# Stream passes that read their tokens from the last to the first, over weight tiles that lie interleaved in pairs

## The chip, the cores and the metric

The kernel runs on one core of a Trainium2 chip. The metric is the device time of one execution in microseconds: the time before is 1301.39 us, the median of three runs (1300.91 to 1302.28).

## The reference

Two layers of a hybrid block over 16 + 256 = 272 tokens of width 1024. Each layer has a mixer (one wide projection, three branches: retention, HGRN2 and differential attention, a gated sum, and an output projection) and a convolutional FFN.

```python
def mixer(hn, w_in, w_branch, w_out, ...):
    proj = (hn @ w_in).astype(F32)             # 1024 -> 13312: the inputs of all branches and the gates
    ...
    o_ret = retention(...); o_hg = hgrn2(...); o_da = diff_attention(...)
    branches = jnp.stack([o_ret, o_hg, o_da], axis=2)
    y_b = jnp.einsum('blnc,ncd->blnd', branches, w_branch.astype(F32))
    gates = jax.nn.sigmoid(mg.reshape(b, l, N_BRANCH, D_MODEL))
    return jnp.sum(gates * y_b, axis=2).astype(hn.dtype) @ w_out

def conv_ffn(hn, w_ffn_in, conv_w, conv_b, w_ffn_out, valid):
    u = jnp.where(valid[None, :, None], hn @ w_ffn_in, 0.0)      # 1024 -> 5632
    ...                                        # a causal convolution of width 3 over tokens
    gate, val = jnp.split(c, 2, axis=-1)
    return (jax.nn.silu(gate) * val) @ w_ffn_out                 # 2816 -> 1024

def reference(x, meta, ...):
    for li in range(DEPTH):                    # 2 layers
        h = h + mixer(rms_norm(h, norm_mix_g[li]), ...)
        h = h + conv_ffn(rms_norm(h, norm_ffn_g[li]), ...)
    return rms_norm(h, norm_final_g)[:, PAD:]
```

Everything is fp32. Nearly all of the arithmetic lies in the products with the weights.

## The kernel before, in words

**The stream.** All weight matrices are cut on the host into tiles of 128 x 128 and laid out in the order in which they are used (`_turns`, `_stream`): 1616 tiles a layer. Eight tiles make a chunk of 512 KB, which one DMA on SP's queue brings into a buffer `wraw` (three of them). ScalarE then rounds the chunk to fp32r (`whi`, four buffers), and VectorE subtracts that from the original to get the rest (`wlo`, four buffers). This is `_Weights.next`. The activations are split in the same way into a high and a low part (`xh`/`xl`, `ghi`/`glo`, `yhi`/`ylo`, `b0hi`/`b0lo` and so on).

**A stream pass.** `products` makes one pair of output column tiles (f = 0 and 1) of a matrix. For each tile it does three matmuls with the weight tile as the stationary operand and the tokens as the moving one (lines 915, 916, 917):

```python
nc.tensor.matmul(o, wh, hi, start=first, stop=False)
nc.tensor.matmul(o, wh, lo, start=False, stop=False)
nc.tensor.matmul(o, wl, hi, start=False, stop=last)
```

Each of them is a weight load of 128 columns (LDWEIGHTS) and a pass of 272 tokens, or of 258 in those parts of the last layer that need no more (`t0` = 14 there). The output `o` lies in PSUM. The two tiles f = 0 and 1 with the same k follow each other in the stream; the exception is the last pair of the first layer's FFN output (`fo`, j = 3), where k follows k. The FFN output of the last layer is computed the other way round: there the weights are the moving operand, 512 wide, and the tokens the stationary one (lines 1520 to 1522).

**Where the tiles lie.** An operand's row k starts at 64 x (k % 4) bytes modulo 256, since a row of 272 tokens has 1088 bytes. `_places` puts each weight tile in its buffer so that its first column, modulo `LINE` = 256 bytes, stands at a set distance `APART` from the operand's row; `APART` has one value for passes of 272 and one for those of 258, and `BLOCK` is added for operands in another kind of buffer. `_runs` joins neighbouring tiles, so that one instruction of ScalarE and one of VectorE does a whole chunk, most often as four runs of 256 columns.

**The order of work.** Every instruction is recorded in a plan (`_Plan`, line 593 is where all recorded calls are issued), and a simulation with fixed costs for each engine orders them once, when the kernel is built. TensorE's stream passes set its clock; the other work (branches, norms, splitting) is spread around them by due times. Most instructions therefore carry line 593 and are told apart by their tiles.

Of the kernel before, what the change touches and what calls it, by code (L numbers as in the profile page):

```python
# [19 lines left out]
P = 128  # L20
DEPTH = 2
# [18 lines left out]
CHUNK_TILES = 8  # L40
# [48 lines left out]
def _ktiles(name):  # L89
    return FK if name == "fo" else KD  # L90


def _turns(li):

    pairs = [x for x in ORDER if x[0][0] not in MARKS]
    if li == DEPTH - 1:
        pairs = [x for x in pairs if x[0] != "fo"]  # L100
    groups = [[x] for x in pairs]
    if li == 0:
        groups[:2] = [pairs[:2]]
    turned = [[pairs[pairs.index((name, 0)) + DEFER - 1]] for name in ("hq", "fi")]
    out = []
    for group in groups:
        if group == [("fo", 3)]:
            out.append([("fo", 3, k, f) for f in range(2) for k in range(FK)])
        else:
            nk = _ktiles(group[0][0])  # L110
            out.append([x + (k, f) for k in range(nk // 2) for x in group for f in range(2)])
            out[-1] += [x + (k, f) for x in group for k in range(nk // 2, nk) for f in range(2)]
            if group in turned:
                out[-1] = out[-1][nk:] + out[-1][:nk]
    if li == DEPTH - 1:
        out.append([("fo", j, k, f) for k in range(FK) for j in range(KD // 2) for f in range(2)])
    return out


STREAM = sum(2 * _ktiles(n) for n, _ in ORDER if n[0] not in MARKS)  # L120


LINE = 256
APART = (0, 200)
BLOCK = 64
ROOM = CHUNK_TILES * P + 2 * LINE // 4
T0 = META - 2
# [3 lines left out]
def _places(depth=DEPTH):  # L131

    wants = []
    for li in range(depth):
        for name, j, k, _ in sum(_turns(li), []):
            if name == "fo" and (li == DEPTH - 1 or j == 3):
                wants.append(None)
                continue  # L140
            short = li == DEPTH - 1 and name not in FULL
            wants.append(APART[short] + BLOCK * (name[0] == "b" or name in ("wo", "fo")) + 64 * (k % 4))
    out = []
    for c in range(0, len(wants), CHUNK_TILES):
        at, places = 0, []
        for want in wants[c : c + CHUNK_TILES]:
            if want is not None:
                at += (want // 4 - at) % (LINE // 4)
            places.append(at)
            at += P  # L150
        assert at <= ROOM
        out.append(places)
    return out


def _runs(places):


    runs = []
    for i, at in enumerate(places):  # L160
        if runs and at == runs[-1][1] + runs[-1][2] * P:
            runs[-1][2] += 1
        else:
            runs.append([i, at, 1])
    out = []
    for i, at, n in runs:
        if out and out[-1][4] == n and (out[-1][3] == 1 or at == out[-1][1] + out[-1][2] * out[-1][3]):
            if out[-1][3] == 1:
                out[-1][2] = at - out[-1][1]
            out[-1][3] += 1  # L170
        else:
            out.append([i, at, 0, 1, n])
    return out
# [22 lines left out]
def _stream(w_in, w_branch, w_out, w_ffn_in, w_ffn_out):  # L196

    out = np.empty((DEPTH, STREAM, P, P), np.float32)
    for li in range(DEPTH):
        tiles = sum(_turns(li), [])  # L200
        for i, (name, j, k, f) in enumerate(tiles):
            if name in BASE:
                w, cols = w_in[li], _columns(name, BASE[name] + 2 * j + f)
            elif name in ("b0", "b1", "b2"):
                w, cols = w_branch[li][int(name[1])], _columns(name, 2 * j + f)
            elif name == "wo":
                w, cols = w_out[li], _columns(name, 2 * j + f)
            elif name == "fi":
                w, cols = w_ffn_in[li], _columns(name, j + f * FK)
            else:  # L210
                w, cols = w_ffn_out[li], _columns(name, 2 * j + f)
            out[li, i] = w[k * P : (k + 1) * P][:, cols]
    n = DEPTH * STREAM // CHUNK_TILES
    out = out.reshape(n, CHUNK_TILES, P, P).transpose(0, 2, 1, 3)
    return np.ascontiguousarray(out).reshape(n, P, CHUNK_TILES * P)
# [382 lines left out]
class _Weights:  # L598
# [13 lines left out]
    def next(self):  # L612
        c, i = divmod(self.used, CHUNK_TILES)
        self.used += 1
        if i == 0:
            due = self.plan.key
            room = [P, ROOM]
            raw = self.plan.tile(self.pool, [P, CHUNK_TILES * P], F32, "wraw", 3, f"wraw{c}")
            hi = self.plan.tile(self.pool, room, F32R, "whi", 4, f"whi{c}")
            lo = self.plan.tile(self.pool, room, F32R, "wlo", 4, f"wlo{c}")  # L620
            self.plan.key = due - LEAD
            pieces = 1 if c > 1 else 2
            for p in range(pieces):
                n = CHUNK_TILES // pieces
                cols = slice(p * n * P, (p + 1) * n * P)
                self.sp.dma_start(raw[:, cols], self.w[c][:, cols])
                for first, at, step, runs, each in _runs(self.places[c][p * n : (p + 1) * n]):
                    src = raw[:, (p * n + first) * P : (p * n + first + runs * each) * P].rearrange("p (r x) -> p r x", r=runs)
                    self.act.activation(self.part(hi, at, step, runs, each), src, AF.Copy)
                    self.dve.tensor_tensor(out=self.part(lo, at, step, runs, each), in0=src, in1=self.part(hi, at, step, runs, each).bitcast(F32), op=SUB)  # L630
            self.plan.key = due
            self.cut = hi, lo
        hi, lo = self.cut
        at = self.places[c][i]
        return hi[:, at : at + P], lo[:, at : at + P]

    def chunk(self):

        for _ in range(CHUNK_TILES):
            self.next()  # L640
        return self.cut


def build(tc, a, depth=DEPTH, probe=None):
# [7 lines left out]
def _trace(ctx, tc, plan, a, depth, probe):  # L652
# [239 lines left out]
    def products(xs, name, j, t0=0):  # L892

        if name in BASE or name == "fi":
            norm.next()
        if ahead:
            return ahead.pop()
        tiles = turns.pop(0)
        main = lambda: new(mp, [P, 2, 512], F32, "main", 2, "main")[:, :, t0:T]
        ps = {i: main() for i in sorted({x[1] for x in tiles})}  # L900
        to = {x: ps[x[0]][:, x[1], :] for x in {x[1::2] for x in tiles}}
        if (name, j) == ("fo", 3):

            to[j, 1] = main()[:, 1, :]
        cost = 3 * ((T - t0) / 2400 + 0.003)
        left = dict.fromkeys(to, _ktiles(name))
        for _, i, k, f in tiles:
            hi, lo = (x[:, t0:] for x in xs(k))
            begun = left[i, f] < _ktiles(name)
            left[i, f] -= 1  # L910
            plan.key = clock[0]
            wh, wl = weights.next()

            def run(o=to[i, f], wh=wh, wl=wl, hi=hi, lo=lo, first=not begun, last=left[i, f] == 0):
                nc.tensor.matmul(o, wh, hi, start=first, stop=False)  # L915
                nc.tensor.matmul(o, wh, lo, start=False, stop=False)  # L916
                nc.tensor.matmul(o, wl, hi, start=False, stop=last)  # L917

            plan.main.append(plan.add("pe", run, cost, [to[i, f]], [wh, wl, hi, lo], count=6))
            clock[0] += cost  # L920
        plan.key = clock[0] - 1.0
        if (name, j) == ("fo", 3):
            return [to[j, f] for f in range(2)]
        ahead.extend(ps[i] for i in ps if i != j)
        return ps[j]
# [71 lines left out]
    for li in range(depth):  # L997
# [546 lines left out]
        for name, j in ORDER:  # L1544
# [18 lines left out]
            elif name[0] == "*":  # L1563
                plan.key = clock[0] - MARGIN
                n = name[1:]
                if n == "b2":
                    blocks = [st["da0"], st["da1"]]
                else:
                    t = st["rg" if n == "b0" else "hg"]
# [4 lines left out]
            two = slice(2 * (j % 2), 2 * (j % 2) + 2)  # L1574
            both = slice(2 * j, 2 * j + 2)
            if name in BASE:
                lo = 0 if name in FULL else t0
# [17 lines left out]
                elif name in ("dq", "dk"):  # L1595
                    t = block(f"{name}{j // 2}")
# [3 lines left out]
                elif name == "rv":  # L1600
# [3 lines left out]
                    src = values(ps, st["rvt"][j // 2], (j % 2) * 2 * P)  # L1604
# [4 lines left out]
                elif name in ("hi", "dv"):  # L1609
                    n = name[0] + "v"  # L1610
# [6 lines left out]
                    src = values(ps, st[f"{n}t{b}"], (j % 2) * 2 * P)  # L1617
# [6 lines left out]
                else:  # L1624
                    t = block(f"{name}{j // 2}")
# [21 lines left out]
            elif name == "wo":  # L1647
                hi, lo = st["yhi"], st["ylo"]
# [11 lines left out]
            elif name == "fi":  # L1660
# [11 lines left out]
                first = META if last else 0  # L1672
                c = temp2("two_b")
                for f in range(2):
# [4 lines left out]
                    for back in (1, 2):  # L1679
                        at = max(first, back)  # L1680
                        stt(c[:, f, at:], u[:, f, at - back - t0 : T - back - t0], w(2 - back), c[:, f, at:], MUL, ADD)
                c = c[:, :, first:]
# [6 lines left out]
            else:  # L1689
                hi, lo = st["ghi"], st["glo"]  # L1690
# [35 lines left out]
```

## Time and profile before

| | |
|---|---|
| median of three runs | 1301.39 us |
| profiled execution, span from its first to its last instruction | 1299.9 us |
| TensorE busy | 1290.8 us (99%) |
| weight loads busy | 1268.7 us (98%) |
| VectorE busy | 993.4 us (76%) |
| ScalarE busy | 855.9 us (66%) |
| GpSimd busy | 85.6 us (7%) |
| DMA | 219.01 MB, mean 168 GB/s |

The profile is of one execution. No time of its own is given for it beside the span; the span is 1.5 us less than the median of the runs. In the rows, PE is TensorE's matmuls, PEld its weight loads, DVE VectorE, ACT ScalarE, POOL GpSimd and SP the engine that issues the weights' DMAs. A group's row has the line, the engine, the operation, output<-inputs, the array's rows x columns, the tile, the count, busy us, the mean ns of one, and the idle time just before. A matmul's duration is longer than the distance to the next one, because matmuls are pipelined: 290 ns and some 125 ns here. A window's row has, for each engine, its busy time and the number of its instructions, then the granted clock, the DMA engines' share and GB/s.

### The profile page before, as it was taken

The numbers are of one execution on the slowest core, as the hardware profiler recorded it, in microseconds if no ns is written. First come the engines' busy times: TensorE is split into PE (matmuls) and PEld (weight loads), VectorE is DVE, ScalarE is ACT, GpSimd is POOL, SyncE is SP. The second block draws the span as 40 slices with busy tenths as digits, with TensorE's granted clock in tenths as the row PEclk, the third lists the DMA queues.
The fourth block names the chain that finished last, engine by engine and source line by source line (L and its number), as shares of the span: only waits on it lengthen the run. The fifth ranks groups of instructions, "written<-read, shape, count | busy, mean of one in ns | idle before, by whom it ended". The sixth has DMA issues, their size and how long they took to land.

```text
span 1299.9 us, 27225 instructions
## 1 busy us (share of the span) xinstructions
PE 1290.8 (99%) x10965; PEld 1268.7 (98%) x10965; DVE 993.4 (76%) x1745; ACT 855.9 (66%) x1490; POOL 85.6 (7%) x162
## 2 busy tenths in 40 slices
PE   9999999999999999999999999999999999999998
PEld 8999999999999999999999999999999999999986
DVE  7685888698686789886565868886997868899753
ACT  6765565766777568776456664657667876787743
POOL 5000000000100020000020000000001100200000
PEclk9999999999999999999999999999999999999999
DMA  8555444435544555555555455454444456556653
GB/s 279 195 159 155 167 149 154 146 136 158 162 143 152 180 161 184 187 173 170 178 179 181 161 171 171 146 172 140 149 161 163 146 163 197 173 186 202 201 183 109
DMA packets 60751, 219.01 MB, mean 168 GB/s; under 512 B 6864, under 2 KB 6992, under 8 KB 60624
## 3 DMA queue, kind: packets, MB, share of 16 engines
q1 hardware_dynamic: 60336, 216.74, 51.6%
q8 instruction: 86, 1.41, 0.4%
q10 hardware_dynamic: 288, 0.52, 0.1%
q14 instruction: 41, 0.34, 0.1%
HBM read 216.19 MB, written 1.05 MB: 167 GB/s over the span
## 4 chain that ended last, share of the span: by engine, by line
PE 95%; DVE 3%; DMA 1%; issue 0%; SPq 0%; POOL 0%; ACT 0%; DVEq 0%
PE main L917 28%; PE main L915 28%; PE main L916 27%; PE fo L1520 2%; PE fo L1522 2%; PE fo L1521 2%; PE ds L1383 1%; PE do L593 1%; PE ro L593 1%; PE ho L593 1%; DMA wraw<-in_w 1%; PE vt L593 1%; DVE wlo L593 1%; PE wt L593 0%; PE lev L1106 0%; PE ms L593 0%
## 5 line engine op out<-in xcount | busy, mean ns | idle before, releaser
L915 PE MATMUL main<-xh,whi 128*128 128x272 f32 (+1 forms) x2368 | 687.8, 290 | 0.7 <-ACT whi L593 0.7
L917 PE MATMUL main<-xh,wlo 128*128 128x272 f32 (+1 forms) x2368 | 679.5, 287 | 0.5 <-DVE wlo L593 0.4
L916 PE MATMUL main<-xl,whi 128*128 128x272 f32 (+1 forms) x2368 | 670.4, 283 | 0.0
L593 DVE TENSOR_TENSOR wlo<-wraw,whi 128x1024 fp32r<-128x1024 f32 (+1 forms) x408 | 496.0, 1222 | 198.7 <-ACT whi L593 195.4
L593 ACT ACTIVATE whi<-wraw 128x1024 fp32r<-128x1024 f32 (+1 forms) x408 | 426.5, 1048 | 214.0 <-PE main L916 137.5
L916 PEld LDWEIGHTS main<-xl,whi 128*128 128x128 f32 x2368 | 449.3, 190 | 0.2
L915 PEld LDWEIGHTS main<-xh,whi 128*128 128x128 f32 x2368 | 445.5, 188 | 2.1 <-ACT whi L593 0.9
L917 PEld LDWEIGHTS main<-xh,wlo 128*128 128x128 f32 x2368 | 444.6, 188 | 1.4 <-DVE wlo L593 1.4
L593 DVE SCALAR_TENSOR_TENSOR two_b<-u,small,two_b 128x256 f32<-128x256 f32 (+2 forms) x176 | 78.3, 485 | 0.7 <-ACT two_b L593 0.2
L593 POOL TENSOR_TENSOR y<-h,rstd 128x272 f32<-128x272 f32 x32 | 38.2, 1225 | 311.1 <-ACT rstd L593 311.1
L917 PE MATMUL main<-ghi,wlo 128*128 128x272 f32 x176 | 51.0, 290 | 0.0
L915 PE MATMUL main<-ghi,whi 128*128 128x272 f32 x176 | 50.8, 288 | 0.0
L916 PE MATMUL main<-glo,whi 128*128 128x272 f32 x176 | 50.2, 285 | 0.0
L593 ACT ACTIVATE two_b<-u,small 128x272 f32<-128x272 f32 (+1 forms) x88 | 49.3, 598 | 0.7 <-DVE glo L593 0.5
L593 ACT ACTIVATE u<-main 128x544 f32<-128x544 f32 (+1 forms) x40 | 24.5, 612 | 36.5 <-PE main L917 36.4
L915 PE MATMUL main<-b0hi,whi 128*128 128x272 f32 (+1 forms) x128 | 37.3, 292 | 0.0
L915 PE MATMUL main<-b1hi,whi 128*128 128x272 f32 (+1 forms) x128 | 37.3, 292 | 0.0
L917 PE MATMUL main<-yhi,wlo 128*128 128x272 f32 (+1 forms) x128 | 36.5, 286 | 0.0
L917 PE MATMUL main<-b2hi,wlo 128*128 128x272 f32 (+1 forms) x128 | 36.5, 285 | 0.0
L917 PE MATMUL main<-b0hi,wlo 128*128 128x272 f32 (+1 forms) x128 | 36.5, 285 | 0.0
L917 PE MATMUL main<-b1hi,wlo 128*128 128x272 f32 (+1 forms) x128 | 36.5, 285 | 0.0
L915 PE MATMUL main<-b2hi,whi 128*128 128x272 f32 (+1 forms) x128 | 36.4, 284 | 0.0
(268 smaller groups left out, 1951.7 us busy)
## 6 DMA issues: line engine op xcount, KB each, us to landing
wraw<-in_w SPq DMA_DIRECT2D x402, 512.0 KB, 3.6
h<-in_h SPq DMA_DIRECT2D x4, 272.0 KB, 5.3
dec<-in_dec SPq DMA_DIRECT2D x2, 544.0 KB, 4.5
wraw<-in_w SPq DMA_DIRECT2D x4, 256.0 KB, 5.0
const<-in_const SPq DMA_DIRECT2D x1, 937.0 KB, 6.8
gain<-in_gl SPq DMA_DIRECT2D x1, 512.0 KB, 5.1
out<-y ACTq DMA_DIRECT2D x2, 256.0 KB, 2.7
out<-y SPq DMA_DIRECT2D x2, 256.0 KB, 2.7
```

Source lines behind the costliest of these rows:

```text
L593: self.plan.add(self.name, lambda: f(*args, **kw), cost, outs, ins, args[2] if method == "activation" else None, count)
L915: nc.tensor.matmul(o, wh, hi, start=first, stop=False)
L916: nc.tensor.matmul(o, wh, lo, start=False, stop=False)
L917: nc.tensor.matmul(o, wl, hi, start=False, stop=last)
L1383: nc.tensor.matmul(ss[m][:, at : at + nk], q[half, hd, q0 : q0 + P], k[half, hd, :nk], start=True, stop=True)
L1520: nc.tensor.matmul(o, gh, wh, start=False, stop=False)
L1521: nc.tensor.matmul(o, gl, wh, start=False, stop=False)
L1522: nc.tensor.matmul(o, gh, wl, start=False, stop=end)
```

## The change

The moving operand's two parts and the output of a stream pass are given to the matmul with step -1, so that the pass walks from the last token to the first and writes each result to the same place as before. On the host, each two neighbouring tiles of the stream are interleaved column by column: column c of the first tile, column c of the second, column c + 1 of the first, and so on. A weight tile is thus read with a step of two elements, 8 bytes. Tiles are placed in pairs rather than singly, and `APART` becomes 80 bytes for both kinds of pass. The weights of the last layer's `fo` keep their layout, and its passes are as before.

```diff
-APART = (0, 200)
+APART = (80, 80)
 ...
-        for want in wants[c : c + CHUNK_TILES]:
+        for want in wants[c : c + CHUNK_TILES : 2]:
             if want is not None:
                 at += (want // 4 - at) % (LINE // 4)
             places.append(at)
-            at += P
+            at += 2 * P
 ...
-        if runs and at == runs[-1][1] + runs[-1][2] * P:
+        if runs and at == runs[-1][1] + runs[-1][2] * 2 * P:
 ...
             out[li, i] = w[k * P : (k + 1) * P][:, cols]
+            mixed[li, i] = name != "fo" or li < DEPTH - 1
+    out, mixed = out.reshape(-1, 2, P, P), mixed.reshape(-1, 2)[:, 0]
+    out[mixed] = out[mixed].transpose(0, 2, 3, 1).reshape(-1, P, 2, P).transpose(0, 2, 1, 3)
 ...
-                for first, at, step, runs, each in _runs(self.places[c][p * n : (p + 1) * n]):
-                    src = raw[:, (p * n + first) * P : (p * n + first + runs * each) * P].rearrange("p (r x) -> p r x", r=runs)
+                for first, at, step, runs, each in _runs(self.places[c][p * n // 2 : (p + 1) * n // 2]):
+                    first, each = p * n + 2 * first, 2 * each
+                    src = raw[:, first * P : (first + runs * each) * P].rearrange("p (r x) -> p r x", r=runs)
 ...
-        hi, lo = self.cut
-        at = self.places[c][i]
-        return hi[:, at : at + P], lo[:, at : at + P]
+        at, f = self.places[c][i // 2], i % 2
+        return [t[:, at : at + 2 * P].rearrange("p (c two) -> p two c", two=2)[:, f, :] for t in self.cut]
 ...
+def backwards(t):
+
+    return bass.AP(t.tensor, t.offset + t.shape[1] - 1, [list(t.ap[0]), [-1, t.shape[1]]])
 ...
             def run(o=to[i, f], wh=wh, wl=wl, hi=hi, lo=lo, first=not begun, last=left[i, f] == 0):
+                o, hi, lo = (backwards(x) for x in (o, hi, lo))
                 nc.tensor.matmul(o, wh, hi, start=first, stop=False)
```

More of the change, by code (lines that the diff above doesn't have):

```diff
@@ L198, in _stream @@
     out = np.empty((DEPTH, STREAM, P, P), np.float32)
+    mixed = np.ones((DEPTH, STREAM), bool)
     for li in range(DEPTH):
```

## The prediction, made before the changed kernel was run

> **What bounds the kernel now.** I read the page first (busy times and the chain that ended last), then the groups by form for TensorE, then the same for its weight loads, then windows inside single stages, and last a piece of the timeline.
>
> The page:
>
> ```profile
> span 1299.9 us, 27225 instructions
> PE 1290.8 (99%) x10965; PEld 1268.7 (98%) x10965; DVE 993.4 (76%) x1745; ACT 855.9 (66%) x1490; POOL 85.6 (7%) x162
> PEclk9999999999999999999999999999999999999999
> PE 95%; DVE 3%; DMA 1%; issue 0%; SPq 0%; POOL 0%; ACT 0%; DVEq 0%
> ```
>
> TensorE is 95% of the chain, at full clock from end to end, and it waits for nobody for long. So the time is a number of passes times the distance from one pass to the next, and only an edit that changes that distance changes the time. The span, 1299.9 us, stands 1.5 us below the median of the runs, 1301.4; I take that difference as fixed and count from the median.
>
> How many passes of the kind that is edited, and how long each stays in the array (groups by form; the last two numbers ahead of the second bar are busy us and mean ns):
>
> ```profile
> L915 PE MATMUL main<-xh,whi 128*128 128x272 f32 x1536 | 450.5, 293 | 0.7 <-ACT whi L593 0.7
> L917 PE MATMUL main<-xh,wlo 128*128 128x272 f32 x1536 | 446.0, 290 | 0.5 <-DVE wlo L593 0.4
> L916 PE MATMUL main<-xl,whi 128*128 128x272 f32 x1536 | 436.7, 284 | 0.0
> L916 PE MATMUL main<-xl,whi 128*128 128x258 f32 x832 | 233.7, 281 | 0.0
> L917 PE MATMUL main<-ghi,wlo 128*128 128x272 f32 x176 | 51.0, 290 | 0.0
> L1520 PE MATMUL fo<-whi,ghi 128*128 128x512 f32 x88 | 34.7, 394 | 0.0
> L915 PE MATMUL main<-b0hi,whi 128*128 128x272 f32 x64 | 19.0, 296 | 0.0
> L915 PE MATMUL main<-b0hi,whi 128*128 128x258 f32 x64 | 18.4, 287 | 0.0
> L593 PE MATMUL ho<-at,vt 128*128 128x144 f32 x32 | 6.5, 286 | 0.0
> L593 PE MATMUL do<-wts,vt 128*128 128x128 f32 x32 | 6.2, 274 | 0.0
> L593 PE MATMUL do<-wts,vt 128*128 128x272 f32 x16 | 5.0, 393 | 0.0
> ```
>
> Three lines (915, 916, 917) each run 1536 + 176 + 4 x 64 = 1968 passes of 272 tokens (b0, b1, b2 and y are the four groups of 64, of which b0 is shown) and 832 + 4 x 64 = 1088 of 258. That is 5904 and 3264 passes, 9168 together. The final fo passes (512 wide) are not touched by the edit.
>
> How far apart they start, in stages where nothing else runs on TensorE (windows; TensorE's count is the first x):
>
> ```profile
> 450.00:600.00 150.00, 150.00 (x1205) 150.00 (x1205) 126.81 (x205) 109.66 (x178) 9.64 (x8) 1.00 0.55 176
> 480.00:520.00 40.00, 40.00 (x323) 40.00 (x322) 39.82 (x67) 32.52 (x56) 6.61 (x6) 1.00 0.53 171
> 520.00:560.00 40.00, 40.00 (x323) 40.00 (x322) 33.12 (x58) 30.28 (x49) 0.00 (x0) 1.00 0.56 179
> 600.00:680.00 80.00, 80.00 (x647) 80.00 (x647) 48.14 (x60) 40.39 (x55) 4.59 (x4) 1.00 0.54 173
> 1100.00:1200.00 100.00, 100.00 (x849) 100.00 (x848) 91.05 (x148) 77.68 (x130) 9.68 (x8) 1.00 0.59 189
> 1120.00:1160.00 40.00, 40.00 (x341) 40.00 (x340) 39.08 (x67) 33.00 (x57) 6.59 (x6) 1.00 0.55 174
> ```
>
> 150 us / 1205 = 124.5 ns for a pass of 272; 100 us / 849 = 117.8 ns for one of 258.
>
> **Is there anything to gain in a pass?** [...] Shape, clock and number of readings are the same on the three lines, so what differs between 284 and 293 are the addresses. VectorE is busy 60% of the time in 600:680 and 83% in 520:560, ScalarE 50% and 76%, and the passes are 123.6 and 123.8 ns apart: the other engines' use of the memory does not make the excess. What remains is TensorE's own second reader, the weight load:
>
> ```profile
> L916 PEld LDWEIGHTS main<-xl,whi 128*128 128x128 f32 x2368 | 449.3, 190 | 0.2
> L917 PEld LDWEIGHTS main<-xh,wlo 128*128 128x128 f32 x2368 | 444.6, 188 | 1.4 <-DVE wlo L593 1.4
> L1106 PEld LDWEIGHTS lev<-extra,hf 128*32 128x32 f32 x256 | 3.8, 110 | 0.6
> ```
>
> 96 columns more cost 188 - 110 = 78 ns: 0.81 ns a column, 1.2 columns/ns, some 104 ns of reading for a tile. The timeline shows that the load of the next tile begins together with the pass it hides under:
>
> ```profile
> 520.26 0.29 PE L915 MATMUL main<-xh,whi 128*128 128x272 f32 x1
> 520.26 0.19 PEld L916 LDWEIGHTS main<-xl,whi 128*128 128x128 f32 x1
> 520.38 0.28 PE L916 MATMUL main<-xl,whi 128*128 128x272 f32 x1
> ```
>
> [...]
>
> **The change, part by part.**
>
> *Step -1 on operand and output, step 2 in the weights.* [...]
>
> The excess is 124.5 - 115.9 for 272, with 115.9 as the distance less the 8.6 ns by which the rows 293, 290, 284 (mean 289, of which some 1 ns is passes that waited) overrun 279.3. For 258 I take 8.0, 117.8 - 109.8, from rows of 281 to 287 against 273.4. All of it gone: 5904 x 8.6 + 3264 x 8.0 = 50.8 + 26.1 = 76.9 us. That is one end. [...] The other end of what a pass keeps is the best row there is, L916, which overruns by 284 - 279.3 = 4.7 ns though its streams cross as well. I let a pass keep 2 ns, a little under the middle of 0 and 4.7, for the moment in which the streams find their distance: 9168 x 2 = 18.3 us stay, 58.6 go.
>
> *Nothing else moves.* The order of instructions on all five engines and the DMA queues is the same before and after; the splitting of a chunk into whi and wlo has the same count and shapes, since the interleaving is already in the stream on the host; each DMA stays 512 KB. The weights of the last fo stay as they are.
>
> *Cover that gets thinner.* VectorE has 39.82 of 40 us to do in 480:520 and 39.08 in 1120:1160, where the norm is folded. At some 117.9 and 111.8 ns a pass TensorE would want these stretches in 323 x 0.1179 = 38.1 and 341 x 0.1118 = 38.1 us. VectorE's work is then late by 1.7 + 1.0 us, less what the four buffers of split weights bridge. Elsewhere it has room (33.12 of 40 in 520:560; 91.05 of 100 in 1100:1200 against 94.9 then). I charge 2.6 us.
>
> Sum: 1301.4 - 58.6 + 2.6 = 1245.4, say **1245 us**. Bounds of this case: 1301.4 - 76.9 = 1224.5 with nothing kept, 1301.4 - 9168 x (8.4 - 4.7) ns + 2.6 = 1270 with all of L916's overrun kept.
>
> **The rivals.**
>
> *The streams keep distance only in part.* [...] A quarter to half of 76.9 us gone, less the charge: 1266 to 1285. Chance 0.14.
>
> *The excess is no meeting of streams.* Then all stays at 1301. For it: no row shows the two readers stall one another, the link is by elimination. Against it: the three lines differ by address alone. Chance 0.05. [...]
>
> *The load at 8 bytes a column is slower.* This is the one that ends on the other side. [...] For it: nothing in this trace loads with a step other than one column. Against: nothing either, so it is 0.10.
>
> *A descending operand or output streams at half rate.* [...] Chance 0.05, milder forms included. [...]
>
> **How the numbers follow.** Forecast 0.66, partial 0.14, nothing 0.05, slower 0.15. The range runs from 1222 (2 us under the floor) through the partial case to no change, 1302; it leaves out the slower cases, 0.15, and a little below. A measurement here can tell 0.2%, 2.6 us. Faster by more 0.80, within 0.05, slower 0.15.
>
> **What would show it.** In the trace after, the three pass lines should fall to one value near 281 to 282 ns for 272 and 275 to 276 for 258, whatever the line, with LDWEIGHTS still at 188; 150 us inside the first FFN should hold some 1270 passes. LDWEIGHTS well over 188 would show the slower load; passes near 393 the half rate. If passes get shorter and TensorE's idle time before L917 grows by DVE wlo, VectorE took the gain back. Rows that still differ by 5 ns between lines, or no change in them, would prove the step on crossings wrong.

## The result, and the profile after

| | before | after |
|---|---|---|
| median | 1301.55 us (4 runs, 1300.91 to 1302.28) | 1307.53 us (4 runs, 1307.07 to 1308.00) |
| profiled execution, span | 1299.9 us | 1306.2 us |

The change makes the kernel slower by half a per cent: the ratio is 1.0046, with a 95% interval of 1.0031 to 1.0060. The forecast was 1245 us with a range of 1222 to 1302, so it was wrong in its sign too.

The page of the changed kernel, the lines that answer to those shown of before:

```profile
span 1306.2 us, 27225 instructions
PE 1297.5 (99%) x10965; PEld 1275.7 (98%) x10965; DVE 994.1 (76%) x1745; ACT 854.8 (65%) x1490; POOL 83.8 (6%) x162
PE 95%; DVE 3%; DMA 1%; ACT 0%; issue 0%; SPq 0%; POOL 0%; DVEq 0%
```

Nothing moved to another engine. TensorE is still 95% of the chain, and its own 6.7 us more (1290.8 to 1297.5) are the whole difference. Its groups by form follow; the pass lines 915 to 917 are now 925 to 927, and the last numbers ahead of the second bar are busy us and mean ns:

```profile
L925 PE MATMUL main<-xh,whi 128*128 128x272 f32 x1536 | 450.7, 293 | 0.3 <-ACT whi L597 0.3
L927 PE MATMUL main<-xh,wlo 128*128 128x272 f32 x1536 | 443.0, 288 | 0.5 <-DVE wlo L597 0.4
L926 PE MATMUL main<-xl,whi 128*128 128x272 f32 x1536 | 442.4, 288 | 0.0
L926 PE MATMUL main<-xl,whi 128*128 128x258 f32 x832 | 236.6, 284 | 0.0
L927 PE MATMUL main<-xh,wlo 128*128 128x258 f32 x832 | 236.3, 284 | 0.0
L926 PE MATMUL main<-glo,whi 128*128 128x272 f32 x176 | 50.7, 288 | 0.0
L927 PE MATMUL main<-ghi,wlo 128*128 128x272 f32 x176 | 50.7, 288 | 0.0
L925 PE MATMUL main<-ghi,whi 128*128 128x272 f32 x176 | 50.7, 288 | 0.0
L925 PEld LDWEIGHTS main<-xh,whi 128*128 128x128 f32 x2368 | 461.3, 195 | 1.8 <-ACT whi L597 0.5
```

Two things stand here. The three lines did come together, as the prediction said they would: where only TensorE's own order decides (ghi and glo), all are at 288. (The 293 on L925 is a mean with a tail of longer stays: in the trace nine of ten of these 1536 lie at 287 or 288.) But they met at 288 and 284 and not at 281 and 275: a pass of 272 still stays 9 ns longer than the 279 ns of one whose operand stands still (a run further down), and one of 258 stays 3 ns longer than before (281 to 284). A weight load grew from 188 or 190 ns to 195.

The same in windows, before first, then after (the first x counts TensorE's passes; 500:560 lies in the first FFN with passes of 272, 1120:1180 in the second with passes of 258):

```profile
500.00:560.00 60.00, 60.00 (x483) 60.00 (x482) 52.94 (x93) 47.12 (x78) 0.00 (x0) 1.00 0.57 181
1120.00:1180.00 60.00, 60.00 (x511) 60.00 (x510) 58.09 (x102) 49.13 (x84) 6.59 (x6) 1.00 0.57 183
1240.00:1280.00 40.00, 40.00 (x175) 32.58 (x175) 18.62 (x16) 15.12 (x16) 0.00 (x0) 1.00 0.61 196
```

```profile
500.00:560.00 60.00, 60.00 (x485) 60.00 (x484) 53.05 (x94) 47.41 (x79) 0.00 (x0) 1.00 0.56 182
1120.00:1180.00 60.00, 60.00 (x501) 60.00 (x501) 57.06 (x97) 47.58 (x83) 9.65 (x8) 1.00 0.55 176
```

A window counts every pass that is in the array during any part of it. So the distance from start to start is the window plus one stay (the mean ns of the rows), divided by the count. A pass of 272 went from 60,289/483 = 124.82 to 60,290/485 = 124.31 ns, and one of 258 from 60,282/511 = 117.97 to 60,286/501 = 120.33 ns. Over the kernel: 5904 x -0.5 + 3264 x 2.4 ns = -3.0 + 7.8 = +4.8 us, of the 6.0 us that were measured. All of the loss is in the passes of 258; a window this short can be off by one pass in 500, 0.2 ns on each kind. The starts of all passes that follow each other without a wait, in the two traces, give 124.7 and 124.4 for 272 and 118.1 and 120.3 for 258.

### The profile page after: what moved, and what is told of

It reads as the page before. It is cut to its first block, busy times and chain, and to the rows that moved or that the text cites. A ratio compares the mean times of both kernels' runs of the same rounds, so it can differ in the third digit from the quotient of the medians.

```text
span 1306.2 us, 27225 instructions
## 1 busy us (share of the span) xinstructions
PE 1297.5 (99%) x10965; PEld 1275.7 (98%) x10965; DVE 994.1 (76%) x1745; ACT 854.8 (65%) x1490; POOL 83.8 (6%) x162
## 4 chain that ended last, share of the span: by engine, by line
PE 95%; DVE 3%; DMA 1%; ACT 0%; issue 0%; SPq 0%; POOL 0%; DVEq 0%
PE main L925 28%; PE main L926 28%; PE main L927 28%; PE fo L1532 2%; PE fo L1530 2%; PE fo L1531 2%; PE ds L1393 1%; PE do L597 1%; PE ho L597 1%; PE ro L597 1%; PE vt L597 1%; DVE wlo L597 1%; PE lev L1116 0%; PE wt L597 0%; PE ms L597 0%; DMA h<-in_h 0%
## 5 line engine op out<-in xcount | busy, mean ns | idle before, releaser
L925 PE MATMUL main<-xh,whi 128*128 128x272 f32 (+1 forms) x2368 | 691.2, 292 | 0.3 <-ACT whi L597 0.3
L926 PE MATMUL main<-xl,whi 128*128 128x272 f32 (+1 forms) x2368 | 679.0, 287 | 0.0
L925 PEld LDWEIGHTS main<-xh,whi 128*128 128x128 f32 x2368 | 461.3, 195 | 1.8 <-ACT whi L597 0.5
L927 PEld LDWEIGHTS main<-xh,wlo 128*128 128x128 f32 x2368 | 460.8, 195 | 1.4 <-DVE wlo L597 1.4
L926 PEld LDWEIGHTS main<-xl,whi 128*128 128x128 f32 x2368 | 461.3, 195 | 0.2
L925 PE MATMUL main<-ghi,whi 128*128 128x272 f32 x176 | 50.7, 288 | 0.0
L925 PE MATMUL main<-b1hi,whi 128*128 128x272 f32 (+1 forms) x128 | 37.7, 294 | 0.0
L925 PE MATMUL main<-b0hi,whi 128*128 128x272 f32 (+1 forms) x128 | 37.6, 293 | 0.0
L926 PE MATMUL main<-b2lo,whi 128*128 128x272 f32 (+1 forms) x128 | 36.6, 286 | 0.0
L926 PE MATMUL main<-ylo,whi 128*128 128x272 f32 (+1 forms) x128 | 36.6, 286 | 0.0
L926 PE MATMUL main<-b0lo,whi 128*128 128x272 f32 (+1 forms) x128 | 36.6, 286 | 0.0
L926 PE MATMUL main<-b1lo,whi 128*128 128x272 f32 (+1 forms) x128 | 36.6, 286 | 0.0
```

## The experiments

Each run below differs from the kernel before, unless it says otherwise, and each changes the stream passes alone (the function `run` inside `products`). The kernels that ran once, those with `still`, `cycled`, x_back, short_front and back_front, stand beside runs of the kernel before on the same chip, 1301.3 to 1302.1 us; they can tell a few us, and not one.

**The two halves of the change, apart**

```diff
+                o, hi, lo = (backwards(x) for x in (o, hi, lo))
```

Theory A is the prediction's own: a pass loses time where its addresses meet those of the load under it. Of step -1 alone it wanted 1255 to 1280 us.

> Before with step -1 on operand and output alone; weight tiles as before, 4 bytes a column, APART (0, 200). [...] Theory B (a descending operand or output costs a pass some 8 ns by itself and ate what the missing crossings gave): 272 at 124 or more, 258 at 120, about 1305 to 1330 us. Theory C (the overrun belongs to the width of a pass with one reading per column, the addresses only ripple it): 1298 to 1305 us.

```diff
-APART = (80, 80)
+APART = (0, 200)
-                o, hi, lo = (backwards(x) for x in (o, hi, lo))
```

(this one against the changed kernel)

> The change without its step -1: weights interleaved, 8 bytes a column, operand and output forward, APART (0, 200). [...] Theory A: passes 3 to 8 ns longer than before, 1325 to 1375 us. Theory B: as before, 1298 to 1310 us. Theory C: 1298 to 1310 us. In all of them LDWEIGHTS reads about 195 ns as in the changed kernel if the step alone makes it longer, 188 if the direction did.

Measured: step -1 alone 1309.72 us (ratio 1.0059, 1.0044 to 1.0074), interleaving alone 1325.18 us (1.0180, 1.0163 to 1.0197). Windows of the first, then of the second:

```profile
500.00:560.00 60.00, 60.00 (x483) 60.00 (x483) 52.92 (x92) 47.09 (x79) 0.00 (x0) 1.00 0.57 184
1120.00:1180.00 60.00, 60.00 (x501) 60.00 (x501) 56.90 (x95) 48.26 (x83) 9.65 (x8) 1.00 0.57 175
```

```profile
500.00:560.00 60.00, 60.00 (x475) 60.00 (x474) 53.09 (x95) 46.07 (x78) 0.00 (x0) 1.00 0.58 181
1120.00:1180.00 60.00, 60.00 (x497) 60.00 (x496) 53.51 (x85) 44.95 (x75) 9.69 (x8) 1.00 0.54 174
```

Step -1 alone gives 483 and 501 passes, within two of the changed kernel's 485 and 501, with loads of the old kind (189 and 190 ns). So the 258 passes' loss is there without any interleaving, and theory A, which wanted 1255 to 1280 us, is out. Interleaving alone makes passes longer, to 126.9 and 121.3 ns (2 and 3 ns) and 1325.18 us, the low end of what A expected and more than the 1298 to 1310 us of B and C; but laid under a descending pass it costs nothing (1309.72 to 1307.53, a gain of 2 us if anything). The weight load of the second:

```profile
L926 PEld LDWEIGHTS main<-xh,wlo 128*128 128x128 f32 x2368 | 464.7, 196 | 0.5 <-DVE wlo L597 0.5
```

196 ns in a forward kernel and 195 in the changed one, against 188 to 190 with 4 bytes a column: the step of 8 bytes makes the load some 7 ns longer, under a pass of either direction.

**Which reader carries the overrun**

```diff
+                wh, wl = (still(x) for x in (wh, wl))      # step 0: one address, 128 times
```

> Before with step 0 in the weights of the stream passes: a load reads one address 128 times (the products are wrong, the work is the same in size). [...] Theory A: 272 at 116 ns, 258 at 110 ns, 1222 to 1235 us. Theory B: the same, since nothing descends in the operand. Theory C: the overrun stays, 272 at 120 to 125 ns, 1270 to 1301 us.

```diff
+                hi, lo = (still(x) for x in (hi, lo))      # step 0: one address, 272 or 258 times
```

> Before with step 0 in the moving operand of the stream passes: a pass reads one address 272 times (products wrong, sizes as before). Theory A: 116 and 110 ns, 1222 to 1235 us. Theory C by reading: the same; theory C by writing the output: 272 at 120 to 125 ns, 1270 to 1301 us. Against still_w it tells on which side the overrun lies.

Measured: 1295.14 us with a load that stands still, 1239.97 us with a pass that stands still. Groups by form of the first, and its windows:

```profile
L928 PE MATMUL main<-xh,wlo 128*128 128x272 f32 x1536 | 443.1, 288 | 0.4 <-DVE wlo L593 0.4
L928 PE MATMUL main<-xh,wlo 128*128 128x258 f32 x832 | 231.3, 278 | 0.0
500.00:560.00 60.00, 60.00 (x483) 60.00 (x483) 52.97 (x93) 47.19 (x79) 0.00 (x0) 1.00 0.58 182
1120.00:1180.00 60.00, 60.00 (x521) 60.00 (x520) 58.82 (x108) 50.34 (x86) 2.31 (x2) 1.00 0.58 186
```

and of the second, with a window and the engines of its chain:

```profile
L928 PE MATMUL main<-xh,wlo 128*128 128x272 f32 x1536 | 428.8, 279 | 0.8 <-DVE wlo L593 0.5
L928 PE MATMUL main<-xh,wlo 128*128 128x258 f32 x832 | 228.8, 275 | 0.0
500.00:560.00 60.00, 60.00 (x519) 60.00 (x518) 54.27 (x94) 47.86 (x79) 0.00 (x0) 1.00 0.62 196
PE 86%; DVE 10%; issue 1%; DMA 1%; POOL 0%; SPq 0%; ACT 0%; DVEq 0%; ACTq 0%
```

This is the verdict on the prediction's mechanism. Taking the load's walk away leaves passes of 272 at 288 ns on this line and at 483 in the window, as before; taking the pass's own walk away brings them to 279, the 279.3 of the prediction's sum, or 116.2 from start to start, and the kernel to 1240 us. The overrun of a pass of 272 is real and was sized rightly; it belongs to the operand that streams. So theory B falls as well, though it had fitted the run with step -1 alone: it too wanted 1222 to 1235 us from the still load. Only the passes of 258 gain from a still load, 281 to 278 or 118.0 to 115.7 from start to start.

**Does it matter where the load is?** Passes of 272 read 34 tokens (136 bytes) 8 times, and the load reads one address, once at its tile's start and once 128 bytes beyond it (modulo 256):

```diff
+                if hi.shape[1] == T:
+                    hi, lo = (cycled(x, 34) for x in (hi, lo))       # [0, 8], [1, 34]
+                    wh, wl = (held(x, 32) for x in (wh, wl))         # near: held(x, 0)
```

> Before, where each stream pass of 272 reads the first 34 tokens of its row 8 times over (136 bytes), and every load under it reads one address 128 bytes beyond its tile's start, outside those 136 bytes modulo 256 (products wrong, sizes as before; passes of 258 unchanged). Theory A (the overrun is the two streams meeting): nothing meets, 272 at 115 to 117 ns, 1240 to 1260 us. Theory D (the pass loses time by its own reading whenever it goes on to another piece of its row, wherever the load is): 272 stays at 122 to 126 ns, 1290 to 1302 us.

> The same with the load's one address at its tile's start, which lies inside the 136 bytes modulo 256 that the pass goes over 8 times. Theory A: 5 to 8 meetings under a load, 272 at 123 to 128 ns, 1285 to 1315 us, and over 6 ns longer than with the far address. Theory D: within 1 ns of the far address.

Measured: 1339.82 and 1339.75 us. Windows, far and then near:

```profile
500.00:560.00 60.00, 60.00 (x460) 60.00 (x459) 54.56 (x92) 46.87 (x79) 8.20 (x7) 1.00 0.55 168
```

```profile
500.00:560.00 60.00, 60.00 (x460) 60.00 (x459) 54.55 (x93) 46.87 (x79) 8.10 (x7) 1.00 0.55 168
```

Far and near are the same to the pass. This pair tells less than it was meant to: a tile starts where its operand's row does, modulo 256, and 128 bytes beyond lies token 32, the last but one of the 34, so the far address was outside them only for loads that belong to a next k. What speaks against theory A is the still load above. Neither theory had foreseen that both would be longer than before: 60,295/460 = 131.1 ns. 136 bytes are eight and a half pieces of 16 bytes, so eight rounds read 72 such pieces, and a whole row of 272 tokens reads 68. That suggested a price per piece, and the next four runs ask how large a piece is.

**What the pass pays for**

```diff
+                if hi.shape[1] == T:
+                    hi, lo = (cycled(x, 4) for x in (hi, lo))        # also 16 and 68
```

> Before, where each stream pass of 272 reads the first 4 tokens of its row 68 times over: it never leaves 16 bytes (products wrong; loads and passes of 258 as before). Theory D (a pass loses some 0.5 ns whenever its reading goes on to another piece of 64 bytes, 17 times in a row): 272 at 115 to 117 ns, 1240 to 1258 us. Theory W (each restart of the pattern costs, 0.8 ns by the 34-token run, which took 131 ns with 8 restarts): over 150 ns, over 1450 us. Theory N (a loss with the number of columns, whatever their addresses): 124 to 125 ns, 1300 us.

> The same with the first 16 tokens 17 times: it never leaves 64 bytes. Theory D: 115 to 117 ns, 1240 to 1258 us; if the piece is 16 bytes and not 64, 124 ns as in a full row, 1300 us. Theory W: 125 to 138 ns.

> The same with the first 68 tokens 4 times: 272 bytes, 5 pieces of 64 bytes each time, 20 in all, 3 restarts. Theory D: 125 to 127 ns. Theory W: 127 to 128 ns. Theory N: 124 to 125 ns.

```diff
+                if hi.shape[1] == T:
+                    hi, lo = (cycled(x, 136) for x in (hi, lo))      # [0, 2], [2, 136]: 8 bytes a column
```

> Before, where each stream pass of 272 reads every second token of its row twice over: 8 bytes from column to column, so 17 pieces of 64 bytes twice (products wrong; loads and passes of 258 as before). Theory D: 34 pieces, 131 to 135 ns, 1335 to 1365 us. Theory N: 124 to 126 ns, 1300 to 1310 us.

Measured: 1257.96, 1315.90, 1313.06 and 1999.12 us. One window of passes of 272 from each, in this order:

```profile
500.00:560.00 60.00, 60.00 (x519) 60.00 (x518) 54.25 (x94) 47.72 (x79) 0.00 (x0) 1.00 0.64 196
```

```profile
500.00:560.00 60.00, 60.00 (x475) 60.00 (x475) 54.03 (x95) 46.03 (x79) 0.00 (x0) 1.00 0.57 177
```

```profile
500.00:560.00 60.00, 60.00 (x477) 60.00 (x476) 53.33 (x94) 46.32 (x80) 0.00 (x0) 1.00 0.59 184
```

```profile
780.00:840.00 60.00, 60.00 (x248) 51.26 (x247) 23.24 (x28) 18.12 (x23) 0.00 (x0) 1.00 0.28 88
```

| the pass of 272 reads | pieces of 16 bytes | ns from start to start |
|---|---|---|
| 4 tokens, 68 times | 1 | 116.2 |
| 16 tokens, 17 times | 4, each 17 times: 68 | 126.9 |
| 68 tokens, 4 times | 17, each 4 times: 68 | 126.4 |
| the whole row (before) | 68 | 124.8 |
| 34 tokens, 8 times | 9, each 8 times: 72 | 131.1 |
| every second token, twice | 68, each twice: 136 | 243.7 |

Staying inside 64 bytes saves nothing (126.9 ns), staying inside 16 bytes saves all of it (116.2, as with the pass that stands still), and 68 restarts of the pattern cost nothing, so theories W and N are out, and D stands with a piece of 16 bytes in place of 64, for which it had expected 131 to 135 ns of the last row. Between 68 and 136 pieces a pass grows by (243.7 - 124.8) / 68 = 1.75 ns a piece; 72 pieces would then be 131.8, and 131.1 were measured. Pieces of 32 bytes would be 34, 68 and, for 34 tokens, 40: 3.5 ns each and 145.8 for the 34 tokens, so they are out. The final fo passes, which nobody touched, fit as well: 512 columns are 128 pieces, 124.8 + 60 x 1.75 = 229.8 ns, and the window 1240:1280 above gives 40,394/175 = 230.8. Four columns of a pass that stays in one piece take 4 x 116.2 / 272 = 1.71 ns, just less than a piece. So the time of a stream pass of 272 or 512 goes with the number of its operand's 16-byte pieces, and a plain load under one of 272 does not count (483 passes in 60 us with the load walking and still). Two things stay open. The price makes 68 x (1.75 - 1.71) = 3 of the 8.6 ns of overrun (124.8 - 116.2); some 6 ns a pass are left, and no run here says what they are. And patterns with 68 pieces differ by 2 ns among themselves (124.8, 126.4 and 126.9).

**Where the 258 passes lost their 2 ns**

```diff
+                hi, lo = (backwards(x) for x in (hi, lo))            # the operand alone
```

> Before with step -1 on the operand alone, output forward (so the products stand in reverse order, wrong). Theory B for the output (writing downwards costs): back to 118 ns for 258, about 1300 us. Theories A and D, which know of reading alone: as with both at step -1, 272 at 124 to 125 ns, 258 at 120, 1306 to 1312 us.

Measured: 1309.15 us, as with both at step -1 (1309.72). The output's direction costs nothing that one run can tell.

```diff
-APART = (0, 200)
+APART = (0, 144)
-            hi, lo = (x[:, t0:] for x in xs(k))
+            at = 0 if name in BASE or name == "fi" else t0
+            hi, lo = (x[:, at : at + T - t0] for x in xs(k))
```

> Before, where the passes of 258 of the wide projections and the FFN input (832 of 1088 on each line) read tokens 0 to 257 and not 14 to 271, forward as before, with APART for them 56 bytes less, so that load and pass begin at the same distance (products wrong). They begin at a multiple of 64 bytes. Theory D, the pieces being aligned: these passes lose more evenly, 119 to 121 ns as in the changed kernel, 1303 to 1310 us. Theory A, same distance and same speeds: 117 to 119 ns on average, 1298 to 1304 us. If the direction itself made the 258 passes 2 ns longer in the changed kernel: 117 to 119 ns too.

The same together with step -1 on operand and output:

> Step -1 on operand and output, tiles not interleaved, and the 258 passes of the wide projections and the FFN input read tokens 257 to 0 and not 271 to 14 (products wrong), APART (0, 144). So the half line of 8 bytes comes first in a descending pass, as it does in a forward one before; in the changed kernel it comes last. If the 2 ns that 258 passes lost come from the half line at the end: 117 to 119 ns, and 1300 to 1304 us. If they come from the direction: 120 to 121 ns, 1308 to 1312 us.

Measured: forward 1306.07 us, descending 1309.06 us. Windows of 258 passes, forward and then descending:

```profile
1120.00:1180.00 60.00, 60.00 (x504) 60.00 (x504) 57.16 (x98) 48.24 (x83) 9.57 (x8) 1.00 0.58 183
```

```profile
1120.00:1180.00 60.00, 60.00 (x501) 60.00 (x500) 57.01 (x95) 48.38 (x83) 9.63 (x8) 1.00 0.57 175
```

A row from token 14 begins in the middle of a 16-byte piece, so 258 tokens touch 65 pieces, one of them half. By 1.75 ns a piece that is 124.8 - 3 x 1.75 = 119.6 ns in any order. Forward, with the half piece first, they take 118.0 (before); forward, half piece last, 60,283/504 = 119.6; descending, half piece last, 120.3; descending, half piece first, 120.3. So forward passes gain some 1.6 ns when the half piece comes first, and descending ones do not gain it in either order: the reading offered ahead of the run, that the half piece at the end costs the 2 ns, fell. That the direction costs them is shown, 2.4 ns with the half piece first and 0.7 with it last; why it does is open.

**Load and pass in the changed kernel**

```diff
-APART = (80, 80)
+APART = (208, 208)
```

> The changed kernel with APART (208, 208): load and pass lie 128 bytes further apart, half of the 256 to which tiles are aligned. Theory L (a pass costs 5.5 ns and 1.75 ns for each 16-byte line it reads; where the load lies counts for little): 272 at 124 to 125 ns, 258 at 120, 1306 to 1309 us. Theory A in its last form (the two run at the same speed, but at 80 bytes in each other's way): 116 to 118 and 110 to 112 ns, 1225 to 1250 us, or longer passes if 80 was the better place.

```diff
                 o, hi, lo = (backwards(x) for x in (o, hi, lo))
+                wh, wl = (still(x) for x in (wh, wl))
```

> The changed kernel with step 0 in the weights of the stream passes: the load reads one address (products wrong). Theory L: 272 at 124 to 125 ns, 258 at 119 to 121, 1303 to 1309 us; LDWEIGHTS back at 188 ns. Theory A: the load is out of the way, 116 and 110 ns, 1225 to 1240 us.

Measured: 1307.33 us (ratio to before 1.0039, 1.0025 to 1.0054) and 1306.29 us. Groups of the second:

```profile
L932 PE MATMUL main<-xl,whi 128*128 128x272 f32 x1536 | 442.4, 288 | 0.0
L932 PE MATMUL main<-xl,whi 128*128 128x258 f32 x832 | 234.8, 282 | 0.0
L932 PEld LDWEIGHTS main<-xl,whi 128*128 128x128 f32 x2368 | 447.0, 189 | 0.3
1120.00:1180.00 60.00, 60.00 (x501) 60.00 (x500) 56.67 (x97) 48.25 (x83) 8.98 (x8) 1.00 0.60 183
```

128 bytes more of distance change nothing (1307.53 to 1307.33 us), and even a load that reads one address leaves 272 at 288 ns and takes some 1 us off the whole. The load's place did not count beside a descending pass: the constant that the change tuned does nothing. The window also shows that the loss of the 258 passes is not made by the load: with a load that stands still under both, they take 115.7 ns forward (521 passes in the still load's window) and 120.3 descending (501).

The three runs that came out faster than the kernel before (1295.14, 1257.96 and 1239.97 us) leave out most of an operand's addresses and so compute other products. No version that computes the kernel's own is faster; the runs name what a pass costs, and no way around it was found for an fp32 operand.

## Why the prediction was wrong

- **That TensorE's distance from pass to pass is the time, and that nothing else moves.** Right. The chain is 95% TensorE before and after, and the windows account for 4.8 of 6.0 us.
- **The floor of a pass, 279 ns in the array or 115.9 from start to start, and so an overrun of some 77 us in all.** Right for 272: with a pass that stands still it is 279 ns and 116.2. The 279.3 and 273.4 in the sum were the author's estimate, with half of the 0.836 ns a column that lie between two plain fp32 rows (144 columns at 286 ns, 272 at 393); no run shows that term, and in its place the runs showed stays of 279 and 275 ns, and 116.2 / 272 = 0.427 ns a column, for a pass that stands still. A pass of 258 gave 6 ns (281 to 275) where 8.0 had been put, so that 5904 x 8.6 + 3264 x 6 = 70 us were there, and the kernel takes 1240 us, a gain of 62. The charge for thinner cover, 2.6 us, looks too small by this: VectorE's share of the chain rises from 3% to 10% there. The distances 124.5 and 117.8 leave out the stay by which a window's count is too high; with it they are 124.7 and 118.1, and no overrun in the sum hangs on that.
- **"What remains is TensorE's own second reader, the weight load".** This is the step that failed. It excluded the other engines and then took the only other reader left, without asking whether the pass could be slow by its own reading. The load held still leaves 288 ns; the pass held still removes the overrun. A part of the trace before pointed to it, fo at 512 wide under a load no longer than the others (188 ns): 230.8 ns from start to start are 12 more than 512 columns at 0.427 ns, where a pass of 272 takes 8.6 more (124.8 against 116.2). In place of the load the runs showed the pass's own operand: 1.75 ns for each 16 bytes of it, where four columns that stay in one piece take 1.71.
- **"Shape, clock and number of readings are the same on the three lines, so what differs are the addresses".** It held for the ripple between lines: with step -1 the lines come together at 288. But the ripple was smaller than it was read: 293 on line 915 is a mean with a tail, and nine of ten of its passes lie at 287 to 290, against 282 to 287 on line 916. And the ripple is not the overrun; the mean stayed, 124.8 against 124.3 ns. That the streams cross was the author's estimate, and no run shows a crossing.
- **The 2 ns that a pass keeps while "the streams find their distance".** No run shows the load's speed or its direction, nor two streams that keep a distance; that was the author's estimate, and with it the 2 ns. In their place the runs showed 8.1 ns that a pass of 272 keeps (124.3 against 116.2), and a load that costs a descending pass next to nothing (1307.53 us with it walking, 1306.29 with it still).
- **The rival with the slower load.** The load did become longer, by 7 ns (188 to 195). It decided nothing: with the load still, and back at 189 ns, the changed kernel takes 1306.29 us against 1307.53.
- **The rival with no gain** was the nearest. For passes of 272 a plain load under them does not count: 483 in 60 us with the load walking and with it still. It is not the whole: under forward passes, loads of 8 bytes a column add 2 to 3 ns (124.8 to 126.9, 118.0 to 121.3), and still ones take 2 to 3 off a pass of 258 (118.0 to 115.7).
- **The rival with the descending stream.** Half rate did not come. For 272 it costs nothing (483 passes in 60 us forward and descending); for 258 it costs 2.4 ns, which is the whole loss. No case of the prediction had a price of that size. The output's part in it is nothing that one run can tell: with the output forward the time is 1309.15 us, with it descending 1309.72.

## What to carry to other kernels

When an instruction overruns, test first whether it overruns by itself: hold one operand still (step 0) at a time, which is one line of code, before building a layout around two operands' meeting. Compare the overrun with the length of the instruction: here the part that grew with the width was the instruction's own. A stream pass of 272 here took 1.75 ns for each 16-byte piece of its moving operand, so that a step of two in it was paid in full (243.7 ns for 124.8).

## What the runs showed of the hardware that was not expected

- A stream pass of 272 costs 1.75 ns for each 16-byte piece of its moving operand, where four columns of a pass that stays in one piece take 1.71: 124.8 ns for 68 pieces, 131.1 for 72, 243.7 for 136, and 116.2 for a pass that stays in one piece. Passes with 68 pieces in other patterns took up to 2 ns more, and passes of 258 lie between 115.7 and 121.3 by direction and load, where the price alone gives 119.6.
- A weight load with two columns to 16 bytes takes 195 ns where one with four takes 188 to 190.
- Descending passes are insensitive to the load (1309.72, 1307.53, 1307.33 and 1306.29 us with it plain, interleaved, interleaved and 128 bytes further off, and still), forward ones are not (1325.18, 1301.79 and 1295.14 us with it interleaved, plain and still). The cause was not found.
